# Hybrid decoder block on one core: sixteen column blocks of the input projection as block products in one stretch

## The chip, the core and the metric

The kernel runs on one core of a Trainium2 chip. A core has TensorE (PE, matrix products into PSUM), VectorE (DVE), ScalarE (ACT), GpSimd (POOL), a queue that issues DMAs (SP), and 16 DMA engines. The metric is the device time of one execution in microseconds, as a median over runs. Lower is better.

## The reference, cut to what matters

One layer with 1024 tokens and width 1024. The normed input is projected once into 5376 columns, which feed an attention branch, a recurrent branch (RWKV-7) and two gates; then come the merge, an output projection and an MLP.

```python
u = rmsnorm(h, norm1_gain)
proj = u @ w_in                                   # 1024 x 1024 times 1024 x 5376
q, k, v, r_p, k_p, v_p, w_p, a_p, g_p, gate_a, gate_b = jnp.split(proj, split_at, axis=-1)
y_attn = sliding_window_attention(q, k, v, ...) @ w_branch_attn
y_rwkv = rwkv7_time_mix(r_p, k_p, v_p, w_p, a_p, g_p, ...) @ w_branch_rwkv
mixed = jax.nn.sigmoid(gate_a) * y_attn + jax.nn.sigmoid(gate_b) * y_rwkv
h = h + mixed @ w_out
hidden = jnp.square(jax.nn.relu(rmsnorm(h, norm2_gain) @ w_ff_in))
return h + hidden @ w_ff_out

def step(S, inp):                                 # the recurrence, per head
    sa = jnp.einsum('bhij,bhj->bhi', S, a_t)
    S = S * w_t[:, :, None, :] + sa[..., None] * b_t[:, :, None, :] + v_t[..., None] * k_t[:, :, None, :]
    return S, jnp.einsum('bhij,bhj->bhi', S, r_t)
```

The recurrence runs over 1024 tokens, in eight heads of 64.

## The kernel before

Every float32 factor is split into a high and a low part (`whi`, `wlo` for weights, `uh`, `ul` for the input), and a product takes three matmuls: low by high, high by low, high by high. A split costs one ACT cast and one DVE subtraction.

**Projection blocks.** The input projection goes in blocks of 128 columns. `load_w` (L151) loads a block's weights in two halves of 256 KB and splits them; `proj` (L183) makes one half of the tokens (512) with 8x3 = 24 matmuls in a PSUM tile `ps_m`, so a block has 48. `proj_z` (L195) copies the result out and stores it in DRAM: `z_d` for the r, k and v columns of the four head pairs (12 blocks, `win_ap[8..19]`), `lz_d` for the lora columns (blocks 0 and 1). `gate` (L752) does the same through a Tanh for the 16 gate blocks (`win_ap[20..35]`), which are read again in the merge.

**Stages.** First the norm with blocks 0 and 8 (lora and the first z block). Then `phase1` (L249): z blocks 9 and 10 (`zproj(0)`), k, v and four q blocks with their preparation, then the recurrence in eight units (four head pairs, two halves of the tokens each). Each unit has three parts:
- `unit_e` prepares a unit: token shift, decay, normalisation, the small triangular inverse (a chain of short DVE instructions on `LT`). It reads `z_d` and `wa_d`.
- `unit_m` makes the unit's inverse matrices (`XT`) and `G0`; there is one `G0` buffer, so it starts when the steps of the unit before are done. Its memset of `XT` (L591) runs on POOL.
- `unit_c` (L630) runs eight steps in a chain: `ry` (PE) to `G` (DVE, L646) to `pu` (PE) to `UV` (DVE, L651) to `pd` (PE) to `sbd` (DVE, L664) to the next `ry`; then the output of the unit (`py`, group norm, `y`).

The loop at the end of `phase1` writes `unit_m(n)`, `estage(n+1)` (which is `unit_e`), `unit_c(n)`. Work that belongs to no unit is placed in the same loop: `zproj(p + 1)` with three z blocks per head pair, and by `fill(PLAN[n + 1])` the gate-lora preparation ("g", with block 1), attention blocks ("a", 8 of them, four steps each) and gates ("x", 14 of them). Two more gates (`NTAIL`) stand behind the loop, then the merge of the branches, the output projection, and the MLP. The MLP already multiplies in blocks of two by two with seven products in place of eight (`group`, `split_w`, `up`, `down`, L996).

**Order.** The order of each engine's instructions is fixed at build time by a planner. It takes, for each engine, the ready instruction with the best priority; priority is the order of the program text, moved forward by `tc.high_priority` (3000 for the three parts of a unit). So fillers go wherever the planner sees an engine free, and may run well ahead of their place in the text. At run time an engine takes its instructions strictly in that order.

Of the kernel before, what the change touches and what calls it, by code (L numbers as in the profile page):

```python
# [20 lines left out]
P = 128  # L21
D = 1024
T = 1024
# [14 lines left out]
PLAN = ("k v q q q q", "g", "a", "a", "a a", "a x", "a x x", "a x x", "a x x x x x x x x x")  # L38
NTAIL = 2

# [19 lines left out]
def hybrid_block(ctx, tc, x_ap, xt_ap, win_ap, lora_ap, wbr_ap, wout_ap, wff1_ap, wff2_ap, cst_ap,  # L60
# [10 lines left out]
    pst = ExitStack()  # L71
    pm = pst.enter_context(tc.tile_pool(name="pm", bufs=2, space=PSUM))
    ps2 = pst.enter_context(tc.tile_pool(name="ps2", bufs=2, space=PSUM))
    pqt = ExitStack()
    ps1 = pqt.enter_context(tc.tile_pool(name="ps1", bufs=1, space=PSUM, side="right"))
# [129 lines left out]

    if True:
# [34 lines left out]
    for k in range(NK):  # L241
        dump(f"uh{k}", uh[k].bitcast(F32))
# [6 lines left out]
    def phase1():  # L249
# [189 lines left out]
        def prep_g():  # L439
            proj_z([(win_ap[1], lz_d[1])])  # L440
# [295 lines left out]
        zproj(0)  # L736
        fill(PLAN[0])
        estage(0)
        for n in range(8):
# [3 lines left out]
            if hf == 0 and p + 1 < NPAIR:  # L743
                zproj(p + 1)
# [6 lines left out]

    def gate(i):  # L752
        w = load_w(win_ap[20 + i])
        for hf in range(2):
            ps = proj(w, uh, ul, hf)
            t = upool.tile([P, HALF], F32, tag="gt", name="gt", bufs=2)
            A.activation(out=t, in_=ps, func=AF.Tanh, scale=0.5)
            nc.sync.dma_start(out=gate_d[i][:, hf * HALF:(hf + 1) * HALF], in_=t)
# [174 lines left out]
    def split_w(src, pool=None, tags=("whi", "wlo")):  # L933
        hi, lo = (w_tile(F32R, t) if pool is None else pool.tile([P, NK, 128], F32R, tag=t, name=t) for t in tags)
        with tc.high_priority(offset=HP_F):
            A.copy(out=hi, in_=src)  # L936
            V.tensor_sub(out=lo, in0=src, in1=hi.bitcast(F32))  # L937
        return hi, lo

    w0 = split_w(raw["a11"], hp, ("c21", "c22"))  # L940
# [51 lines left out]
    def group(out, pairs, start):  # L992
        n, last = 0, 3 * len(pairs) - 1
        for (lh, ll), (rh, rl) in pairs:
            for a, b in ((ll, rh), (lh, rl), (lh, rh)):
                PE.matmul(out=out, lhsT=a, rhs=b, start=start and n == 0, stop=n == last, skip_group_check=True)  # L996
                n += 1
# [213 lines left out]
```

## Time and profile before

| | us |
|---|---|
| median of 3 runs | 1529.18 (1528.53 to 1529.93) |
| profiled execution | 1529.62 |
| its span, first to last instruction | 1527.8 |
| PE busy | 1491.3 (98%) |
| PE weight loads busy | 1177.2 (77%) |
| DVE busy | 1044.1 (68%) |
| ACT busy | 639.1 (42%) |
| POOL busy | 192.2 (13%) |

Busy shares are averages over stages. The span has these: norm and first blocks to 77.8 us, k, v and q to 152, the recurrence with fillers to 586, the rest of attention with gates to 642, gates alone to 706, then the merge, the output projection and the MLP to the end. A matmul's record is longer than its share of the engine, since matmuls overlap; what one costs is read from a stretch of many.

### The profile page before, as it was taken

The page shows a single profiled execution, that of the slowest core. Times are in us where ns is not written, and L with a number is a line of the kernel's source. Part 1 is how long each engine was busy: PE and PEld are TensorE (multiplying, and loading weights), DVE is VectorE, ACT ScalarE, POOL GpSimd, SP SyncE. Part 2 cuts the span into 40 slices and gives each one's busy share as a digit, 9 for nine tenths or more (in the row PEclk, how much of TensorE's full clock was granted, in tenths as well). Part 3 has the DMA queues.
Part 4 walks back from the last instruction along what each step waited for, and adds up shares of the span by engine and source line. Part 5 has one row for each costly group of instructions (what it writes and reads, how often), then busy time and mean ns, then how long its engine had stood idle before and what let it go on. Part 6 is the DMA issues. An engine that isn't in the chain of part 4 may idle for free.

```text
span 1527.8 us, 22206 instructions
## 1 busy us (share of the span) xinstructions
PE 1491.3 (98%) x8396; PEld 1177.2 (77%) x8396; DVE 1044.1 (68%) x2056; ACT 639.1 (42%) x1126; POOL 192.2 (13%) x116
## 2 busy tenths in 40 slices
PE   5999999999999999999999999999999999999998
PEld 5878777777777777788888787878787878787776
DVE  4232678888988875353656579595858687776867
ACT  6332436456545665441224354332424333423332
POOL 1000000000000000000000111323223232323230
PEclk9999999999999999999999999999999999999999
DMA  5455334334222323383433111111120111111112
GB/s 192 165 149 146 109 103 149 103 104 120 88 90 66 103 84 124 117 295 113 136 125 146 42 42 56 56 42 69 42 69 28 69 42 65 46 56 42 56 55 111
DMA packets 99771, 145.65 MB, mean 95 GB/s; under 512 B 26448, under 2 KB 48848, under 8 KB 99664
## 3 DMA queue, kind: packets, MB, share of 16 engines
q1 hardware_dynamic: 99664, 144.23, 28.8%
q8 instruction: 66, 1.08, 0.3%
q14 instruction: 41, 0.34, 0.1%
HBM read 108.54 MB, written 35.65 MB: 94 GB/s over the span
## 4 chain that ended last, share of the span: by engine, by line
PE 75%; DVE 19%; ACT 3%; issue 2%; DMA 1%; SPq 0%; DVEq 0%; ACTq 0%
PE ps_m L164 32%; PE psy L996 15%; PE psx L996 12%; DVE wlo L937 4%; DVE c L1021 2%; DVE c L1001 2%; DVE tlo L1032 2%; PE po L164 2%; PE ps_o L927 1%; PE pu L170 1%; DVE h L1094 1%; ACT c L1004 1%; ACT whi L936 1%; PE pk L246 1%; PE ps_s L170 1%
## 5 line engine op out<-in xcount | busy, mean ns | idle before, releaser
L164 PE MATMUL ps_m<-uh,wlo 128*128 128x512 f32 x576 | 235.5, 409 | 0.0
L164 PE MATMUL ps_m<-ul,whi 128*128 128x512 f32 x576 | 234.3, 407 | 0.0
L164 PE MATMUL ps_m<-uh,whi 128*128 128x512 f32 x576 | 233.0, 404 | 0.0
L996 PE MATMUL psy<-T,whi 128*128 128x512 f32 x512 | 159.6, 393 | 0.0
L164 PEld LDWEIGHTS ps_m<-uh,whi 128*128 128x128 f32 x576 | 108.6, 189 | 21.2 <-issue 0.8
L164 PEld LDWEIGHTS ps_m<-uh,wlo 128*128 128x128 f32 x576 | 108.6, 189 | 21.1 <-issue 0.6
L164 PEld LDWEIGHTS ps_m<-ul,whi 128*128 128x128 f32 x576 | 108.7, 189 | 20.2 <-issue 0.7
L996 PEld LDWEIGHTS psy<-T,whi 128*128 128x128 f32 x512 | 96.1, 188 | 21.9
L157 DVE TENSOR_TENSOR wlo<-wraw,whi 128x512 fp32r<-128x512 f32 x101 | 67.9, 687 | 56.6 <-ACT whi L156 56.4
L996 PE MATMUL psx<-tlo,whi 128*128 128x512 f32 x256 | 101.9, 398 | 4.5 <-DVE tlo L1032 4.5
L937 DVE TENSOR_TENSOR wlo<-fraw_a,whi 128x1024 fp32r<-128x1024 f32 x47 | 66.0, 1405 | 57.5 <-ACT whi L936 57.5
L936 ACT CAST whi<-fraw_a 128x1024 fp32r<-128x1024 f32 x47 | 49.3, 1049 | 129.1 <-PE psy L996 85.7
L996 PE MATMUL psx<-thi,wlo 128*128 128x512 f32 x256 | 101.6, 398 | 1.5 <-DVE h L1094 0.9
L996 PE MATMUL psx<-thi,whi 128*128 128x512 f32 x256 | 101.0, 395 | 0.0
L996 PE MATMUL psy<-T,wlo 128*128 128x512 f32 x256 | 100.6, 393 | 0.0
L967 POOL TENSOR_TENSOR fraw_a<-fraw_a,fraw_a 128x1024 f32<-128x1024 f32 x16 | 45.5, 2846 | 346.7 <-DVE s L942 345.5
L1094 DVE TENSOR_TENSOR h<-h,psx 128x1024 f32<-128x1024 f32 (+1 forms) x66 | 76.8, 1179 | 9.6 <-PE psx L996 9.6
L996 PE MATMUL psy<-tlo,whi 128*128 128x512 f32 x192 | 77.2, 402 | 3.1 <-DVE tlo L1032 3.1
L156 ACT CAST whi<-wraw 128x512 fp32r<-128x512 f32 x105 | 61.0, 619 | 45.4 <-PE ps_m L164 45.3
L996 PE MATMUL psy<-thi,wlo 128*128 128x512 f32 x192 | 75.8, 395 | 0.0
L996 PE MATMUL psy<-thi,whi 128*128 128x512 f32 x192 | 75.8, 395 | 0.0
L996 PE MATMUL psy<-B,whi 128*128 128x512 f32 x240 | 74.8, 393 | 0.0
(298 smaller groups left out, 3227.1 us busy)
## 6 DMA issues: line engine op xcount, KB each, us to landing
wraw<-win SPq DMA_DIRECT2D x72, 256.0 KB, 3.3
fraw_a<-wff SPq DMA_DIRECT2D x32, 512.0 KB, 3.2
wraw<-wff SPq DMA_DIRECT2D x32, 512.0 KB, 3.2
gate_d<-gt SPq DMA_DIRECT2D x32, 256.0 KB, 2.0
z_d<-zt SPq DMA_DIRECT2D x24, 256.0 KB, 2.3
xt<-x SPq DMA_DIRECT2D x8, 512.0 KB, 5.7
la<-wa_d SPq DMA_DIRECT2D x8, 512.0 KB, 4.3
aq<-q_d SPq DMA_DIRECT2D x8, 512.0 KB, 4.2
```

Of the source, the lines that this page charges most:

```text
L156: A.copy(out=hi[:, ks], in_=raw[:, ks])
L157: (eng or V).tensor_sub(out=lo[:, ks], in0=raw[:, ks], in1=hi[:, ks].bitcast(F32))
L164: PE.matmul(out=out, lhsT=a, rhs=b, start=(n == 0), stop=(n == last))
L170: after = PE.matmul(out=out, lhsT=lhsT, rhs=rhs, start=start, stop=stop).ins
L936: A.copy(out=hi, in_=src)
L937: V.tensor_sub(out=lo, in0=src, in1=hi.bitcast(F32))
L967: G.tensor_sub(out=a21, in0=a11, in1=a21)
L996: PE.matmul(out=out, lhsT=a, rhs=b, start=start and n == 0, stop=n == last, skip_group_check=True)
L1001: V.scalar_tensor_tensor(out=c, in0=c, scalar=0.0, in1=r2[:, (lo_, hi_)[hf]].unsqueeze(1).broadcast_to([P, 2, HALF]), op0=ALU.max, op1=ALU ...
L1021: V.tensor_sub(out=C[out], in0=C[a], in1=C[out])
L1032: V.tensor_sub(out=lo, in0=src, in1=hi.bitcast(F32))
L1094: V.tensor_add(out=ht, in0=ht, in1=ps[:, c0 % 2:c0 % 2 + step])
```

## The change

Sixteen of the blocks no longer go through `proj`. They are taken in four groups of four blocks (`GROUPS`): z blocks 9 and 10 with lora block 1 and z block 11; z blocks 12 to 15; z blocks 16 to 19; gates 2 to 5 (blocks 22 to 25). A group is a product of two by two blocks (512 weight rows by 256 columns each, against 512 input rows by 512 tokens), made from seven products P1 to P7 of 24 matmuls in place of 192 matmuls. The weights of a group come in four tiles of 512 KB from a new input `wst`. Sums of weights are made on DVE (`weight`), sums of the input once, on DVE and POOL (`in_sums`), and the products are added up on DVE (`product`). Results go to the same places in DRAM (`out_`).

The stretch stands between the norm stage and `phase1`; gates 0 and 1 go ahead of it as ordinary blocks. The PSUM pools are closed for it and opened again behind it (`psum_pools`). `phase1` loses both uses of `zproj` and block 1 in `prep_g`; `PLAN` keeps eight attention blocks and the gates 6 to 13.

```diff
-PLAN = ("k v q q q q", "g", "a", "a", "a a", "a x", "a x x", "a x x", "a x x x x x x x x x")
+PLAN = ("k v q q q q", "g", "a", "a", "a a", "a x", "a x", "a x", "a x x x x x")
+GROUPS = ((9, 10, 1, 11), (12, 13, 14, 15), (16, 17, 18, 19), (22, 23, 24, 25))
...
+    strassen_order = ("P1", "P5", "P6", "P2", "P7", "P3", "P4")
+    def split_w(src, pool=None, tags=("whi", "wlo"), hp=0):
+        hi, lo = (w_tile(F32R, t) if pool is None else pool.tile([P, NK, 128], F32R, tag=t, name=t) for t in tags)
+        with tc.high_priority(offset=hp):
+            A.copy(out=hi, in_=src)
+            V.tensor_sub(out=lo, in0=src, in1=hi.bitcast(F32))
+        return hi, lo
...
+    def in_sums(wp):
...
+        for k in range(4):
+            E.append(wp.tile([P, 2, HALF], F32, tag=f"c{k}", name=f"e{k}"))
+            for i in range(2):
+                G.tensor_add(out=E[k][:, i], in0=uh[k + 4 * i][:, lo_].bitcast(F32),
+                             in1=ul[k + 4 * i][:, lo_].bitcast(F32))
+        for k in range(4):
+            S.append(wp.tile([P, 2, HALF], F32, tag=f"sm{k}", name=f"s{k}"))
+            for i in range(2):
+                V.tensor_add(out=S[k][:, i], in0=uh[k + 4 * i][:, hi_].bitcast(F32),
+                             in1=ul[k + 4 * i][:, hi_].bitcast(F32))
+        for name, out, x, y in (("T1", (E, 0), (S, 0), (E, 0)), ("T2", (E, 0), (S, 1), (E, 0)),
+                                ("T3", (S, 0), (S, 1), (S, 0)), ("T4", (E, 1), (E, 1), (E, 0))):
+            for k in range(4):
+                o, a, b = (m[k][:, i] for m, i in (out, x, y))
+                V.tensor_sub(out=o, in0=a, in1=b)
+                t = wp.tile([P, T], F32R, name=f"{name}{k}")
+                A.copy(out=t[:, lo_], in_=o)
+                V.tensor_sub(out=t[:, hi_], in0=o, in1=t[:, lo_].bitcast(F32))
...
+    def in_groups(wp, pw, B):
...
+        def weight(g, name):
+            a11, a21, a12, a22 = (raw[g, n] for n in names)
+            w = split_w({"P1": a11, "P5": raw.get("s1"), "P6": a11, "P2": a12, "P7": a21, "P3": raw.get("s4"),
+                         "P4": a22}[name])
+            if name == "P1":
+                raw["s1"] = wp.tile([P, NK, 128], F32, tag="sm0", name="s1")
+                V.tensor_add(out=raw["s1"], in0=a21, in1=a22)
+            elif name == "P5":
+                V.tensor_sub(out=a21, in0=a11, in1=a21)
+                V.tensor_sub(out=a11, in0=raw["s1"], in1=a11)
+            elif name == "P6":
+                raw["s4"] = wp.tile([P, NK, 128], F32, tag="sm1", name="s4")
+                V.tensor_sub(out=raw["s4"], in0=a12, in1=a11)
+                fetch(g + 1, "a11")
...
+        def product(g, name, w):
...
+            for a in range(2):
+                group(ps[:, a], [((hi[:, 4 * a + k], lo[:, 4 * a + k]), B[rhs[name]][k]) for k in range(4)],
+                      name in ("P1", "P5", "P2"))
...
+            if name in ("P1", "P5", "P6", "P4"):
+                C[i, hf] = wp.tile([P, 2, HALF], F32, tag=f"c{2 * i + hf}", name="cw")
+                A.copy(out=C[i, hf], in_=ps)
+            else:
+                V.tensor_add(out=C[i, hf], in0=C[i, hf], in1=ps)
+            if name in ("P2", "P7", "P3", "P4"):
+                out_(g, i, hf)
...
     nst.close()
+    wst = ExitStack()
+    wp = wst.enter_context(tc.tile_pool(name="wspool", bufs=1))
+    for i in range(2):
+        gate(i)
+    B_in = in_sums(wp)
+    pqt.close()
+    pw = [None, wst.enter_context(tc.tile_pool(name="pw1", bufs=1, space=PSUM, side="right"))]
+    pst.close()
+    pw[0] = wst.enter_context(tc.tile_pool(name="pw0", bufs=1, space=PSUM))
+    pw.reverse()
+    in_groups(wp, pw, B_in)
+    wst.close()
+    psum_pools(1)
...
         def prep_g():
-            proj_z([(win_ap[1], lz_d[1])])
...
-        def zproj(p):
-            for i in range(0 if p else 1, 3):
-                proj_z([(win_ap[8 + 3 * p + i], z_d[3 * p + i])])
-
-        cnt = {"q": 0, "a": 0, "x": 0}
+        cnt = {"q": 0, "a": 0, "x": 6}
...
         prep_wa()
-        zproj(0)
         fill(PLAN[0])
...
-            if hf == 0 and p + 1 < NPAIR:
-                zproj(p + 1)
```

## Rows read from the trace of the kernel before

**Rows 1.** The page, part 1: busy us, share of the span, instructions.
```profile
PE 1491.3 (98%) x8396; PEld 1177.2 (77%) x8396; DVE 1044.1 (68%) x2056; ACT 639.1 (42%) x1126; POOL 192.2 (13%) x116
```

**Rows 2.** Busy time by stage; columns named in the first line.
```profile
core 0: us, PE busy (x) PEld busy (x) DVE busy (x) ACT busy (x) POOL busy (x), PEclk, DMA share, GB/s
0.00:77.80 77.80, 61.38 (x288) 51.28 (x288) 29.16 (x63) 39.87 (x65) 7.57 (x19) 1.00 0.49 175
...
152.00:586.00 434.00, 428.19 (x3703) 322.11 (x3703) 358.88 (x1265) 238.59 (x575) 6.77 (x34) 1.00 0.33 103
```

**Rows 3.** The chain that ended last, in order of time: start, length, what.
```profile
642.24 207.91 PE ps_m L164 x902
```

**Rows 4.** Busy time, a stretch of the MLP's products; columns as in rows 2.
```profile
960.00:1060.00 100.00, 98.89 (x425) 79.36 (x424) 68.82 (x52) 33.30 (x33) 31.72 (x12) 1.00 0.15 53
```

**Rows 5.** Instructions on ps_m alone, by stage: PE, PEld, DVE, ACT, clock, DMA.
```profile
152.00:586.00 434.00, 243.37 (x804) 137.82 (x803) 0.00 (x0) 19.41 (x33) 1.00 0.33 103
586.00:642.00 56.00, 43.52 (x166) 29.22 (x166) 0.00 (x0) 4.13 (x7) 1.00 0.31 106
642.00:706.00 64.00, 63.92 (x274) 51.52 (x275) 0.00 (x0) 6.76 (x12) 1.00 0.66 226
```

**Rows 6.** Busy time, the units of the recurrence; columns as in rows 2.
```profile
152.00:246.30 94.30, 91.42 (x609) 66.46 (x610) 66.81 (x222) 45.32 (x95) 0.88 (x8) 1.00 0.36 111
246.30:291.50 45.20, 44.87 (x418) 32.97 (x420) 37.59 (x125) 27.35 (x67) 1.08 (x6) 1.00 0.40 128
291.50:352.90 61.40, 60.36 (x503) 45.38 (x503) 54.19 (x201) 32.74 (x81) 0.99 (x6) 1.00 0.32 95
352.90:397.30 44.40, 44.40 (x427) 33.72 (x425) 40.08 (x147) 26.57 (x63) 1.38 (x7) 1.00 0.39 121
397.30:445.10 47.80, 46.86 (x439) 35.41 (x439) 43.06 (x148) 26.00 (x62) 0.84 (x4) 1.00 0.36 107
445.10:489.50 44.40, 44.30 (x423) 33.29 (x423) 39.71 (x140) 24.83 (x57) 0.98 (x5) 1.00 0.21 64
489.50:537.50 48.00, 47.50 (x458) 36.57 (x456) 41.09 (x156) 27.43 (x78) 0.64 (x2) 1.00 0.31 89
537.50:576.00 38.50, 38.48 (x386) 30.18 (x383) 28.16 (x100) 22.68 (x62) 0.00 (x0) 1.00 0.29 96
```

**Rows 7.** Timeline of POOL, one of six such memsets: start, length, what, [idle before].
```profile
445.12 0.53 POOL L591 MEMSET XT<- 128x512 f32 x1 [29.14 <-DMA XT<-lx_d]
```

**Rows 8.** Timeline, part of a step of the fifth unit.
```profile
434.02 0.28 DVE L651 COPY UV<-pu 64x128 f32<-64x128 f32 x1
...
434.82 0.38 PE L654 MATMUL pd<-UV,BKt 128*128 128x128 f32 x2
...
435.31 0.58 DVE L664 SCALAR_TENSOR_TENSOR sbd<-pd,wc,sw 64x64 f32<-64x64 f32 x2 [0.23 <-PE pd L654]
...
435.96 0.40 PE L164 MATMUL ps_m<-uh,whi 128*128 128x512 f32 x1
...
436.20 0.38 PE L644 MATMUL ry<-sbd,AR 128*128 128x128 f32 x2
436.22 0.75 DVE L422 SCALAR_TENSOR_TENSOR v<-z,vec,v 128x512 f32<-128x512 f32 x1
...
437.00 0.29 DVE L646 TENSOR_TENSOR G<-G,ry 64x128 f32<-64x128 f32 x1
```

**Rows 9.** The UV copies of the fifth and the last unit: ns min/median/max, first and last start.
```profile
L651 DVE COPY UV<-pu x8: 275/289/295, 417.5 to 445.1; 64x128 f32<-64x128 f32 x8
L651 DVE COPY UV<-pu x8: 277/289/295, 552.3 to 575.9; 64x128 f32<-64x128 f32 x8
```

**Rows 10.** Attention's last copy of a step, from 586 us on.
```profile
L395 ACT COPY ya<-po x10: 353/368/369, 587.8 to 642.3; 64x256 f32<-64x256 f32 x10
```

**Rows 11.** Groups by line, 152 to 586 us: busy us, mean ns, idle before.
```profile
L157 DVE TENSOR_TENSOR wlo<-wraw,whi 128x512 fp32r<-128x512 f32 x34 | 23.2, 684 | 0.6 <-ACT whi L156 0.6
```

**Rows 12.** The page, part 5: a sum of weights on POOL.
```profile
L967 POOL TENSOR_TENSOR fraw_a<-fraw_a,fraw_a 128x1024 f32<-128x1024 f32 x16 | 45.5, 2846 | 346.7 <-DVE s L942 345.5
```

More of the change, by code (lines that the diff above doesn't have):

```diff
@@ L204, in proj_z, with gate @@
                 nc.sync.dma_start(out=dst[:, hf * HALF:(hf + 1) * HALF], in_=t)
+    def gate(i):
+        w = load_w(win_ap[20 + i])
+        for hf in range(2):
+            ps = proj(w, uh, ul, hf)
+            t = upool.tile([P, HALF], F32, tag="gt", name="gt", bufs=2)
+            A.activation(out=t, in_=ps, func=AF.Tanh, scale=0.5)
+            nc.sync.dma_start(out=gate_d[i][:, hf * HALF:(hf + 1) * HALF], in_=t)
+    lo_, hi_ = slice(0, HALF), slice(HALF, T)
+    strassen_order = ("P1", "P5", "P6", "P2", "P7", "P3", "P4")
@@ new lines, in split_w, with group @@
+    def split_w(src, pool=None, tags=("whi", "wlo"), hp=0):
[4 more added lines that the diff above has]
+        return hi, lo
+    def group(out, pairs, start):
+        n, last = 0, 3 * len(pairs) - 1
+        for (lh, ll), (rh, rl) in pairs:
+            for a, b in ((ll, rh), (lh, rl), (lh, rh)):
+                PE.matmul(out=out, lhsT=a, rhs=b, start=start and n == 0, stop=n == last, skip_group_check=True)
+                n += 1
@@ new lines, in in_sums @@
+    def in_sums(wp):
+        B = {n: [] for n in ("T1", "T2", "T3", "T4")}
+        E, S = [], []
+        for k in range(4):
[16 more added lines that the diff above has]
+                V.tensor_sub(out=t[:, hi_], in0=o, in1=t[:, lo_].bitcast(F32))
+                B[name].append((t[:, lo_], t[:, hi_]))
+        for name, o, sl in (("B11", 0, lo_), ("B21", 4, lo_), ("B22", 4, hi_)):
+            B[name] = [(uh[o + k][:, sl], ul[o + k][:, sl]) for k in range(4)]
+        return B
@@ L750, in phase1 @@
         st.close()
[L752 to L758, printed above, removed]
     phase1()
@@ L931, in hybrid_block @@
     hp = gst.enter_context(tc.tile_pool(name="hpool", bufs=1, side="right"))
[L933 to L940, printed above, removed]
+    w0 = split_w(raw["a11"], hp, ("c21", "c22"), HP_F)
     s1 = hp.tile([P, NK, 128], F32, tag="c12", name="s1")
@@ L990, in weight @@
         return w
[L992 to L997, printed above, removed]
     def act2(c, hf):
@@ L1167, in _layout @@
     du, au, gu = f("decay_up"), f("aaa_up"), f("gate_up")
+    wst = w.reshape(2, 4, P, -1)[:, :, :, cols[np.array(GROUPS)]]
+    wst = wst.reshape(2, 4, P, len(GROUPS), 2, 2, P).transpose(3, 5, 0, 2, 4, 1, 6)
+    wst = np.ascontiguousarray(wst.reshape(len(GROUPS), 4, P, 8, P)[:, [0, 2, 1, 3]])
     lora = np.stack([np.concatenate([du, au]), gu])
```

63 lines of the change are left out of this document (51 added, 12 removed).

## Prediction

> **What bounds the kernel now.** I read the busy shares first, then the stages, then the recurrence unit by unit, then one step of it. TensorE (PE) is busy for 98% of the span [rows 1], so at first sight fewer matmuls mean less time. The stages say what that is made of [rows 2]. Once the input is there, up to 152 us, and from 642 us on PE works through projections without a gap; 902 of them in a row take 207.91 us, 0.2305 us each [rows 3]. Between 152 and 586 us runs the recurrence, eight units (four head pairs, two halves each). There PE is also full, but 804 of its 3703 matmuls are projections (ps_m) that have nothing to do with the unit being worked on [rows 5]: z columns for later pairs, the gate-lora block, gates. At 0.2305 us they are 185 us of the 434. They are fillers: PE does them while the chain of the recurrence waits for VectorE (DVE), ScalarE or a DMA. So the question here is not how many matmuls there are but how long the recurrence is without them.
>
> The units are marked by a memset on POOL that waits for the last step of the unit before [rows 7]; by these marks the periods are 45.2, 61.4, 44.4, 47.8, 44.4 and 48.0 us, then 38.5 for the last [rows 6]. DVE is busy for 90% of the third, fourth and fifth of these and for 73% of the last one, which alone has no following unit to prepare. A step of the chain goes pd (PE), sbd (DVE), ry (PE), G (DVE), pu (PE), UV (DVE). In [rows 8] UV starts at 434.02 and lasts 0.28, and pd starts only at 434.82, behind three fillers; sbd ends near 435.89 and ry starts at 436.20, behind one; ry is through near 436.6 and G waits until 437.00, behind a 0.75 us DVE instruction of the next unit's preparation. Both engines delay the chain, and a step takes (445.1-417.5)/7 = 3.9 us; in the last unit, with PE just as full and DVE freer, (575.9-552.3)/7 = 3.4 [rows 9].
>
> **The change, part by part.** All sums are against the profiled execution, 1529.62 us with a span of 1527.8, so 1.8 us outside it; the median is 1529.18, 0.4 lower.
>
> *Front swap.* z blocks 1 and 2 leave the stretch ahead of 77.8 us, gates 0 and 1 come in: 96 matmuls against 96, nothing.
>
> *New stretch.* Four groups of seven products of 24 matmuls, 672 for 768. The stage that works in the same product form runs 425 matmuls in 100 us, 0.2353 each with its own stalls [rows 4]: 158 us. Added to that is the hand-over of PSUM and SBUF at both ends, which no row shows. It lies between nothing (two banks are free before the last eviction) and one eviction with its store, some 6 us, since k's first projection is queued behind it on PE and v and q behind that; I take 4, nearest to the idle that the product stage shows per 100 us (1.1). Together 162 us. The sums of the input cost DVE 40 instructions at 684 ns [rows 11], 27 us, and POOL eight of half the 2846 ns form [rows 12], 11 us. They lie beside the two gates (22 us of PE) and the first products, and need only the input that exists by about 40 us; nothing, or, with that cover gone, up to 10 us for the first two sums. Per group seven splits and seven sums go to DVE, some 18 of 40 us, as in the product stage, and SP carries 512 KB weight loads in place of 256 KB ones: hidden.
>
> *What leaves.* Between 152 and 706 us there are 804+166+274 = 1244 recorded projections, 1248 by count (10 z and lora blocks, 16 gates of 48). 480 stay, 768 go: 177 us of PE. So the stage of 554 us could fall to 377 if PE stayed full, and the kernel gains by 554-377-162 = 15 us. It breaks even where the stage takes 392 us.
>
> *What the stage takes instead.* Ten blocks leave with 20 DVE splits of 684 ns [rows 11], 1.7 us per unit. (ACT loses as many casts and as many evictions; it is busy for 239 of 434 us [rows 2] and binds nowhere. SP loses 20 loads and 20 stores there, and gets 16 larger loads and 32 stores in the stretch.) DVE is busy about 40 us in a full period [rows 6]; 38.3 at the same 90% is a period of 42.5. The delay by fillers, about half a microsecond per step in [rows 8], points the same way (3.9 to 3.4, or 4 us per unit). The 61.4 us period, in which the preparation of unit 2 came late behind its own z blocks, and the 48.0 become 42.5 as well. The bounds are 38.5 (the last unit) and 45. The first unit, 94.3 us with DVE at 71%, is a chain of small work and DMA round trips: 88, between 80 and 94. The last period stays at 38, the output of the last unit at 10, from its last step [rows 9] to 586 us. Recurrence: 88+6x42.5+38+10 = 391 us for 434.
>
> Behind it, before, ten of 32 attention steps were left, at one step every 6 us (587.8 to 642.3 [rows 10]), and gates filled PE around them and until 706. Attention is filler too and needs the DVE that the recurrence needs. It can start some 60 us earlier in the first unit, as no z blocks stand ahead of it, but the rest is shorter; I take six steps left, 36 us (between 10 and 56). The two tail gates (22 us) fit beside them. Then the last attention block must be stored, loaded and split before the merge: 6 us with no gate left to hide it (0 to 11). The eight gates in the plan are low priority, and whether they run early or late does not alter the chain.
>
> Stage: 391+36+6 = 433 us, so 121 less; the new stretch costs 162. Result +41: 1527.8+41+1.8-0.4, rounded 1570 us.
>
> A rule of the Trainium skill speaks against the change: Perfetto Trace Analysis, § Optimization Strategy, says that where the most-contended engine changes between regimes, interleaving the regimes can help. The change takes two interleaved regimes apart. The trace agrees as far as [rows 2] show both engines full in one stage (PE 428 and DVE 359 of 434 us); the sum above does not use the rule.
>
> **The rivals.**
>
> *Fillers set the pace (faster).* The order on each engine is fixed when the program is built, and in [rows 8] PE matmuls that could wait stand ahead of chain matmuls twice in one step. If that is most of why a step takes 3.9 us, the freed recurrence runs at 36 us per unit or less: 88+7x36+10 = 350, attention ends beside it, and the stage meets PE's own bound, 377: 1514 us. The point is a period of 36 with a tail of 42 us, or 39.5 with one of 17. Against it: no period in the trace is under 38.5, and that one had DVE at 73%.
>
> *Between.* Periods of 39 to 41 and attention mostly done: a stage of 395 to 415, 1530 to 1550.
>
> *DVE has the last word (slower still).* The work does not fall, periods stay at 45 and all ten attention steps remain: 94+6x45+38+10+56+11 = 479, 1616 us.
>
> *A lower clock.* The granted clock is 1.00 in every stretch shown [rows 2, 6]. In all but the first of them PE is over 95% busy; in the first, ahead of 77.8 us, it is busy for 79%, still at 1.00, which speaks against this rival, though there the idle time lies mostly before the first matmul. After the change PE has at most 434-185+88 = 337 us of work (the 88 for eight gates) in 391. If the granted clock fell to the lower level (1.2 GHz) in the recurrence, three matmul groups per step and four per unit preparation would each lengthen by some tenths of a microsecond, 20 to 60 us in all: 1590 to 1630. The Trainium skill, TensorE: Matmul & The Clock Gate, Part 1, says that the array runs at half rate by default and at full rate only while it is kept busy. By that rule the recurrence would be where it falls; no row here shows it, and the forecast does not contain it.
>
> *It doesn't do what it says.* The count (96 matmuls fewer) follows from the loops; I give this no chance.
>
> **How the numbers follow.** Forecast (1550 to 1595): 0.56. Fillers set the pace, 1510 to 1526: 0.15. Between, 1526 to 1550: 0.16, of which 0.04 lies within 0.2% of 1529.2. DVE or clock, over 1595: 0.13. About 0.2%, 3 us, is what a measurement of this kernel can tell from no change. So faster 0.15, same 0.04, slower 0.81. The range goes from the PE bound, 1514, to near the upper sum, 1612; the forecast's own is 1550 to 1595.
>
> **What would show it.** Right: the stretch with products lasts about 162 us with PE full; POOL's marks in the recurrence are 41 to 44 us apart with DVE at 88 to 92%; PE there is clearly under 90% busy and waits for DVE; attention runs on after the last unit with few ps_m beside it. Wrong: marks under 38 us apart, or PE still full to the end of attention (fillers set the pace); granted clock under 1.00 in the recurrence; a product stretch over 170 us, in which case the hand-over or the input sums were not hidden.

## Result, and the profile after

The change makes the kernel slower: 1637.79 us (median of 4 runs, 1633.61 to 1639.25) against 1528.87 for the kernel before, a ratio of 1.0705 [1.0689, 1.0721]. The forecast was 1570 with a range to 1612; the sign was right and the size was not, by 68 us.

The profiled execution has a span of 1637.4 us. Two lines of its page, to be read beside [rows 1], first the busy shares, then TensorE's granted clock in 40 slices of 41 us:

```profile
PE 1529.0 (93%) x8300; PEld 1209.8 (74%) x8300; DVE 1116.4 (68%) x2120; ACT 661.8 (40%) x1130; POOL 205.2 (13%) x124
...
PEclk9999998957778999998599999999999999999999
```

There are 96 matmuls fewer (8396 to 8300 recorded), and PE is busy for 38 us more. The second line says where: the clock dips in slice 7 (the hand-over from the stretch to k), in slices 9 to 13 (the first units of the recurrence) and in 19 and 20 (the way into the merge). Before, it was 1.00 everywhere it was looked at [rows 2, 6].

The same by stage: the new stretch, k/v/q, the first unit, the seven others by their last step, the rest of attention, the start of the merge. Columns: window, length, busy us (and count) of PE, its weight loads, DVE, ACT, POOL, then granted clock, DMA share, GB/s.

```profile
71.00:229.30 158.30, 157.87 (x687) 128.75 (x686) 69.33 (x61) 47.94 (x53) 0.00 (x0) 1.00 0.26 95
229.30:322.50 93.20, 85.84 (x391) 68.34 (x389) 26.68 (x69) 26.88 (x49) 2.35 (x12) 0.93 0.55 153
322.50:440.10 117.60, 91.72 (x545) 68.55 (x546) 82.89 (x308) 64.02 (x160) 0.87 (x8) 0.67 0.33 101
440.10:488.70 48.60, 41.96 (x370) 33.09 (x372) 36.15 (x132) 24.11 (x57) 1.09 (x6) 0.72 0.22 67
488.70:548.10 59.40, 53.54 (x463) 41.32 (x463) 51.82 (x186) 32.74 (x84) 0.97 (x6) 0.91 0.35 107
548.10:595.20 47.10, 46.82 (x443) 35.46 (x441) 43.38 (x154) 27.48 (x65) 1.23 (x7) 1.00 0.33 100
...
738.00:777.70 39.70, 37.34 (x334) 29.40 (x335) 26.53 (x93) 23.82 (x67) 0.00 (x0) 0.87 0.18 64
777.70:797.00 19.30, 2.98 (x37) 2.42 (x37) 6.66 (x21) 2.70 (x5) 0.00 (x0) 0.50 0.24 83
797.00:818.00 21.00, 11.04 (x20) 5.31 (x21) 13.45 (x12) 7.31 (x7) 0.00 (x0) 0.58 0.88 310
```

Before, the same stages are, in one line each: k/v/q 82.0 us, first unit 93.4, the seven others together, the tail:

```profile
71.00:153.00 82.00, 81.72 (x398) 65.44 (x396) 25.27 (x67) 22.99 (x44) 0.10 (x1) 1.00 0.54 147
153.00:246.40 93.40, 90.52 (x608) 66.08 (x609) 65.91 (x220) 45.40 (x95) 0.94 (x9) 1.00 0.35 111
246.40:575.90 329.50, 326.56 (x3018) 247.33 (x3016) 283.75 (x1010) 187.40 (x465) 5.83 (x26) 1.00 0.33 100
575.90:705.50 129.60, 128.80 (x645) 102.91 (x646) 54.25 (x145) 59.65 (x140) 0.00 (x0) 1.00 0.49 167
```

Four marks divide the time in every kernel below: the first `th` activation (the recurrence begins), the last `UV` copy of the eighth unit, the merge's first matmul, the end. "Recurrence" is first `th` to last `UV`, "stage" is first `th` to the merge's first matmul, "rest" is from there to the end of the last instruction that counts as busy work.

| kernel | us | first th | first unit | recurrence | stage | rest |
|---|---|---|---|---|---|---|
| before | 1528.9 | 153.0 | 93.4 | 423.0 | 552.6 | 819.0 |
| after | 1637.8 | 322.5 | 117.6 | 455.2 | 474.5 | 837.4 |
| plain | 1648.5 | 330.8 | 117.4 | 455.6 | 474.9 | 838.1 |
| minus10 | 1491.9 | 152.4 | 116.0 | 454.8 | 518.1 | 818.8 |
| minus10_warm | 1529.0 | 153.5 | 90.2 | 420.4 | 551.7 | 818.9 |
| nofill | 1651.1 | 151.2 | 119.5 | 493.3 | 677.3 | 818.8 |
| warm | 1657.9 | 322.0 | 90.9 | 422.9 | 495.5 | 836.5 |
| warm8 | 1654.3 | 320.9 | 91.3 | 438.1 | 489.6 | 838.2 |
| noattn | 1640.8 | 323.5 | 104.8 | 457.0 | 476.5 | 836.8 |
| early | 1668.7 | 324.3 | 110.6 | 463.7 | 506.4 | 836.9 |
| hold3 | 1655.9 | 318.0 | 117.9 | 467.0 | 510.3 | 820.4 |
| g1 | 1553.9 | 209.5 | 94.3 | 426.7 | 510.9 | 830.8 |
| gates6 | 1560.8 | 220.7 | 92.5 | 423.2 | 497.9 | 837.3 |
| g1g | 1556.9 | 218.9 | 92.4 | 421.7 | 495.6 | 836.3 |

So after against before is +169.5 in front, -78.1 in the stage, +18.4 in the rest: 109.8 by the trace, 108.9 by the medians. 768 matmuls, 177 us at 0.2305, left the stage, and less than half of that time came back. The recurrence didn't shorten; it grew by 32 us.

Those 32 us aren't spread evenly: 24 of them lie in the first unit, ahead of its first step. From the first `th` to the first `UV` copy it is 90.9 us for 67.2 before; the eight steps take 26.7 for 26.2. More attention lies there too. A step of attention ends with one `ya` copy: the first unit holds nine of them, for one before, and the whole recurrence all 32, for 21. Both kinds of copy in the first unit, before and then after (ns min/median/max, first and last start, shapes):

```profile
L395 ACT COPY ya<-po x1: 366/366/366, 237.2 to 237.2; 64x256 f32<-64x256 f32 x1
L651 DVE COPY UV<-pu x8: 277/289/296, 220.2 to 246.4; 64x128 f32<-64x128 f32 x8
```

```profile
L533 ACT COPY ya<-po x9: 365/366/367, 335.6 to 439.2; 64x256 f32<-64x256 f32 x9
L788 DVE COPY UV<-pu x8: 281/288/295, 413.4 to 440.1; 64x128 f32<-64x128 f32 x8
```

### The profile page after: what moved, and what is told of

It reads as the page before. It is cut to its first block, busy times and chain, and to the rows that moved or that the text cites. A ratio compares the mean times of both kernels' runs of the same rounds, so it can differ in the third digit from the quotient of the medians.

```text
span 1637.4 us, 22102 instructions
## 1 busy us (share of the span) xinstructions
PE 1529.0 (93%) x8300; PEld 1209.8 (74%) x8300; DVE 1116.4 (68%) x2120; ACT 661.8 (40%) x1130; POOL 205.2 (13%) x124
## 4 chain that ended last, share of the span: by engine, by line
PE 35%; DVE 12%; ACT 2%; issue 2%; DMA 1%; ACTq 0%; DVEq 0%
PE psy L233 14%; PE psx L233 11%; PE ps_m L169 9%; DVE wlo L226 3%; DVE c L1128 2%; DVE c L1108 2%; DVE tlo L1139 2%; PE ps_o L1049 1%; DVE h L1201 1%; ACT c L1111 1%; ACT whi L225 1%; DVE c L1176 1%; DVE c L1172 1%; DMA gg<-g_d 0%; DMA yt<-ya_d 0%
## 5 line engine op out<-in xcount | busy, mean ns | idle before, releaser
L169 PE MATMUL ps_m<-uh,wlo 128*128 128x512 f32 x320 | 134.1, 419 | 2.5 <-DVE wlo L162 2.5
L169 PE MATMUL ps_m<-ul,whi 128*128 128x512 f32 x320 | 133.7, 418 | 0.0
L169 PE MATMUL ps_m<-uh,whi 128*128 128x512 f32 x320 | 132.4, 414 | 0.0
L233 PE MATMUL psw<-T,whi 128*128 128x512 f32 x256 | 79.0, 390 | 0.0
L169 PEld LDWEIGHTS ps_m<-uh,wlo 128*128 128x128 f32 x320 | 61.9, 194 | 13.9 <-DVE wlo L162 2.9
L1138 ACT CAST thi<-c 128x1024 fp32r<-128x1024 f32 x56 | 58.7, 1048 | 32.2 <-DVE c L1128 31.9
L169 PEld LDWEIGHTS ps_m<-uh,whi 128*128 128x128 f32 x320 | 61.9, 193 | 11.7 <-issue 0.2
L169 PEld LDWEIGHTS ps_m<-ul,whi 128*128 128x128 f32 x320 | 62.0, 194 | 11.1 <-issue 0.9
```

The costliest lines, as they stand in the source:

```text
L169: PE.matmul(out=out, lhsT=a, rhs=b, start=(n == 0), stop=(n == last))
```

## The experiments

Three theories stood at the start. A: PE without projections between the chain's small matmuls loses its clock, and that lengthens the chain. B: the load of DVE and attention sets the length of a unit. C: matmuls that stand ahead of the chain's own slow it.

**warm: the kernel after, with the missing PE work put back as matmuls that nothing reads.**

```diff
+    def warm(n):
+        for j in range(n):
+            ps = pm.tile([P, HALF], F32, tag="m", name="ps_w")
+            sl = slice(j % 2 * HALF, (j % 2 + 1) * HALF)
+            mm3(ps, [((uh[k][:, 0:128], ul[k][:, 0:128]), (uh[k][:, sl], ul[k][:, sl])) for k in range(NK)])
...
         def prep_g():
+            warm(2)
...
+            if hf == 0 and p + 1 < NPAIR:
+                warm(6)
```

> The changed kernel with 480 matmuls added in the recurrence, at the places where the ten blocks stood before. They multiply slices of the input by each other into PSUM and nobody reads the result, so TensorE is given back its filler without a split, a copy or a DMA; the output is the same. Theory A (the granted clock, low from 315 to 490 us and at the entry of the merge, makes the first units long): the clock returns to 1.00, the stretch from the first tanh of unit 0 to POOL's first mark falls from 118 us to about 95, the marks at 488 and 548 come 45 us apart, and the total falls by 40 us or more, to 1590 or less. Theory B (VectorE's queue sets the units, filler or not): the clock returns, the first stretch gives back at most 10 us, the marks stay 47 us apart, 1615 to 1635. Theory C (matmuls standing ahead of the chain slow it): slower than 1640.

Measured: 1657.9 us, ratio 1.0842 [1.081, 1.0873]. The recurrence is 422.9, that of the kernel before to 0.1 us, though no work was added but that of PE. The window view of its first unit and of the seven others:

```profile
322.00:412.90 90.90, 88.94 (x613) 64.77 (x612) 63.70 (x206) 38.99 (x82) 1.40 (x9) 1.00 0.27 84
412.90:744.90 332.00, 328.19 (x2998) 249.10 (x2998) 277.07 (x1004) 174.71 (x445) 5.12 (x25) 0.99 0.25 77
```

Against the kernel after, the first unit is 27 us shorter, at a clock of 1.00 for 0.67. But the planner, with PE full, also put attention elsewhere: the first unit holds one of its steps and no longer nine, as in the kernel before, and the first step of the unit comes 65.7 us after the first `th`:

```profile
L539 ACT COPY ya<-po x1: 365/365/365, 406.4 to 406.4; 64x256 f32<-64x256 f32 x1
L795 DVE COPY UV<-pu x8: 272/288/295, 387.7 to 412.9; 64x128 f32<-64x128 f32 x8
```

So warm shows that the missing PE work is what lengthened the recurrence, but not by itself whether through the clock or through the place of attention. The total missed theory A's 1590 by 68 us and lies where theory C had it: attention was pushed behind the recurrence (its last copy starts at 808.8, for 775.7), so the stage is 495.5 for 474.5. A shorter recurrence that is paid with pushed work wins nothing.

**noattn: the kernel after without attention** (zeros are stored in its place).

```diff
-                for g in range(2):
-                    pend.append(attn_s(blk, hh, g))
-                    if len(pend) > 1:
-                        attn_o(pend.pop(0))
+                ya = ap.tile([P, 2, 128], F32, tag="ya", name="ya")
+                G.memset(ya, 0.0)
+                nc.sync.dma_start(out=ya_d[:, 2 * hh:2 * hh + 2, b * 128:(b + 1) * 128], in_=ya)
```

> The changed kernel without the attention steps; zeros are stored in their place, so VectorE loses about 5 to 10 us of work in each unit and 19 us in the first, TensorE and ScalarE lose theirs too. Theory B (VectorE's load sets the period): the marks on POOL come about 41 us apart in place of 47, the first stretch falls from 118 to under 100 us, total 1560 to 1585. Theory A (clock): with still less work on TensorE the clock falls further, the first units stay long, total 1610 or more. If the dependence chain of a unit itself takes 45 us, the marks stay at 45 to 47 and the total is 1600 to 1630.

Measured: 1640.8 us, ratio 1.073 [1.0699, 1.0761]; the recurrence is 457.0. The first unit, and the last two, which have neither attention nor projections beside them:

```profile
323.50:428.30 104.80, 71.48 (x435) 51.27 (x434) 66.22 (x208) 39.06 (x72) 2.41 (x13) 0.66 0.29 89
...
678.80:736.00 57.20, 35.86 (x304) 27.11 (x305) 31.67 (x103) 10.66 (x26) 0.65 (x2) 0.56 0.10 24
736.00:780.50 44.50, 29.52 (x263) 22.21 (x263) 17.36 (x55) 8.41 (x23) 0.00 (x0) 0.50 0.02 7
```

In the last one DVE is busy for 17.36 of 44.50 us, nothing competes with the chain, and it still takes longer than the last unit of the kernel before (38.5 us with DVE at 28.16 [rows 6]). So B doesn't explain this unit. DVE's load isn't without effect, though. Units 4 to 6 run at a clock of about 1.00 with and without attention; they take 137.9 us here and 142.1 in the kernel after, 4 us less for 11 us less of DVE's work (noattn, then after):

```profile
540.90:678.80 137.90, 134.06 (x1220) 96.47 (x1218) 115.91 (x373) 61.69 (x131) 2.94 (x14) 0.99 0.25 79
548.00:690.10 142.10, 141.05 (x1321) 106.23 (x1323) 127.23 (x453) 82.01 (x198) 3.40 (x15) 1.00 0.30 92
```

And the first unit is 13 us shorter than after's at about the same clock (0.66 for 0.67), all of it ahead of the first step, which comes 76.8 us after the first `th`, for 90.9:

```profile
L784 DVE COPY UV<-pu x8: 282/289/295, 400.3 to 428.4; 64x128 f32<-64x128 f32 x8
```

So at the low clock the nine attention steps cost the first unit 13 us, about half of what it had grown by. Theory B had it under 100 us, and theory A had it stay long: it lies between. The later units, which lost attention as fill too, gave the 13 us back.

**minus10: the kernel before without ten of its blocks, and without the stretch.** The nine z blocks of the later pairs and lora block 1 aren't computed; all pairs read the columns of the first blocks.

```diff
         def prep_g():
-            proj_z([(win_ap[1], lz_d[1])])
...
-            if hf == 0 and p + 1 < NPAIR:
-                zproj(p + 1)
```

> The kernel before with the ten blocks of the recurrence simply left out (every head pair reads the z columns of the first pair, the gate lora those of the other lora); no new stretch, gates and attention as before. It is the removal alone. If units run faster without filler, as I forecast (periods of 42.5 us), the stage from 152 us to the merge meets TensorE's own bound of 443 us: 1418 us, periods 42 or less. Theory B (VectorE sets the units): periods stay at 44 to 47, gates are used up as filler, the stage takes 470 to 500 us and the total is 1445 to 1475. Theory A adds a low clock in the first unit, and then the total lies at the upper end or above it.

Measured: 1491.9 us, ratio 0.9757 [0.972, 0.9793]. Ten blocks are 480 matmuls, 110.6 us of PE, and leaving them out altogether is worth 37; my own forecast for this run, 1418 us with periods of 42 or less, missed by 74. The recurrence (454.8) is that of the kernel after (455.2) without anything of the stretch: what lengthens it is that the blocks left the recurrence, with all that the planner then moved: here too the first unit holds nine attention steps and the recurrence all 32.

**minus10_warm: the same with 480 matmuls that nothing reads in the blocks' places**; `warm` as above, in the old places of `proj_z` and `zproj`.

> The kernel before without the ten blocks (the four pairs read the first blocks' columns, as in the run without them), and in their places 480 matmuls of the same size whose results nothing reads: TensorE is busy as before, but there are no weight fetches, splits, evictions and stores. Clock theory: the recurrence is back at 423 us, against 455 without the matmuls, and the whole kernel is at 1529, give or take 8: TensorE's work is the whole of the difference of 37 us between the kernel before and the one without the blocks. Rival (the ten blocks cost by their evictions, stores and splits on VectorE and ScalarE): the recurrence stays under 423 and the kernel ends at 1492 to 1515. If PE's work comes in full on top of 1492 (110 us at full clock for 480 matmuls), 1600.

Measured: 1529.0 us, ratio 1.0004 [0.9993, 1.0015], as the clock theory had it. The work that this kernel has and minus10 hasn't is PE's alone: no weight fetch, split, copy or store. The order differs further: with the PE work back, the planner again puts one attention step in the first unit and 21 in the recurrence. The first unit and the seven others, of minus10:

```profile
152.40:268.50 116.10, 91.28 (x547) 68.66 (x548) 82.96 (x308) 63.94 (x160) 0.91 (x9) 0.68 0.33 102
268.50:607.10 338.60, 324.72 (x2951) 248.81 (x2950) 281.69 (x1007) 187.07 (x470) 5.84 (x26) 0.94 0.29 87
```

and of minus10_warm:

```profile
153.50:243.70 90.20, 88.68 (x613) 64.83 (x612) 63.56 (x207) 39.11 (x82) 1.40 (x9) 1.00 0.27 85
243.70:573.90 330.20, 326.45 (x2998) 247.79 (x2999) 276.74 (x1004) 174.94 (x445) 5.12 (x25) 1.00 0.26 77
```

Two readings. More work on PE made the recurrence 34 us shorter, with the clock at 1.00 for 0.68 and 0.94 and with eleven attention steps fewer in it. And against the kernel before, which has its attention in the recurrence in the same number (21 steps), the ten blocks' twenty splits and all their copies are gone from DVE and ACT, and the recurrence is 420.4 for 423.0: that relief is worth 2.6 us, not the 42 that the prediction gave it.

**nofill: minus10 with every gate block held behind the last unit.**

```diff
-                    gate(i)
+                    with tc.issue_after(held[0]):
+                        gate(i)
```

> The kernel before without the ten blocks, and with all gate blocks held until the last unit's output matmul, so that the recurrence has no projection work at all beside attention in its early units (the four pairs read the first blocks' columns). Clock theory: the units that have nothing beside them run at a granted clock of 0.5 to 0.6 and steps of 3.8 to 4.1 us, so first tanh to last mark is 475 to 500 us, against 455 with gates and 423 with gates and blocks, and the whole kernel is slower than the 1491.9 without the hold by more than 20 us plus the held gates that no longer hide. Rival (filler competes with the recurrence): the recurrence shortens to 390 to 440.

Measured: 1651.1 us, ratio 1.0803 [1.0762, 1.0844]; the recurrence is 493.3, within the 475 to 500 of the clock theory; the rival wanted 390 to 440.

```profile
151.20:270.70 119.50, 87.91 (x504) 65.93 (x505) 83.48 (x311) 62.01 (x156) 0.87 (x8) 0.62 0.30 90
270.70:644.50 373.80, 301.43 (x2482) 236.22 (x2483) 272.12 (x985) 169.57 (x432) 5.66 (x26) 0.63 0.19 53
```

This run parts the clock from attention, which lies as in minus10: nine steps in the first unit, 31 in the recurrence for 32. The first unit, at 0.62 for 0.68, is 3.5 us longer, and the seven others, at 0.63 for 0.94, are 35 us longer, though the gates' splits and copies are gone from DVE and ACT.

A clock of 0.63 is a mean of stretches at 1.00 (2.4 GHz) and at 0.50 (1.2 GHz). The chain's `pd` matmul shows what that is for one instruction (ns min/median/max, first and last start, shapes), first here, then in minus10_warm:

```profile
L653 PEld LDWEIGHTS pd<-UV,BKt x120: 186/331/338, 242.3 to 641.2; 128*128 128x128 f32 x120
L653 PE MATMUL pd<-UV,BKt x120: 275/421/583, 242.3 to 641.4; 128*128 128x128 f32 x120
```

```profile
L660 PEld LDWEIGHTS pd<-UV,BKt x120: 186/188/193, 219.0 to 570.9; 128*128 128x128 f32 x120
L660 PE MATMUL pd<-UV,BKt x120: 269/273/378, 219.2 to 571.0; 128*128 128x128 f32 x120
```

Weight load and matmul each take some 145 ns more. Eight steps and the unit's preparation are made of such small matmuls, each waited for: the seven later units take 373.8/7 = 53.4 us each, for 48.4 in minus10 and 47.2 in minus10_warm. From no fill to full fill the recurrence is 493.3, 455, 420 to 423; the last of these differences holds the shift of attention too.

**plain: the sixteen blocks in the same place in front, as plain block products.**

```diff
+    for i in range(6):
+        gate(i)
+    for s, d in [(win_ap[1], lz_d[1])] + [(win_ap[8 + i], z_d[i]) for i in range(1, 12)]:
+        proj_z([(s, d)])
```

> The sixteen column blocks stand in the same place in front, but as plain block products: no input sums, no sevenths, none of the new memory; the recurrence's fill is that of the kernel after. The stretch is then sixteen blocks of 48 matmuls, 16 x 48 x 0.2305 = 177 us, where the change's is 158. If the 11 us between the stretch and the k block are the hand-over of the change's memory, they are gone: first tanh at 153 + 177 = 330, against 322.5, recurrence 455, merge entry as after, and the whole kernel is at 1645, give or take 7. Rival (the seven products save what they were meant to, and the 11 us have another cause): first tanh 341, whole kernel 1656. If the block products themselves are what slows the kernel (the recurrence's length has to do with what stood in front), the recurrence is at 423 and the kernel at 1613 or less.

Measured: 1648.5 us, ratio 1.0788 [1.0757, 1.082], first `th` at 330.8, recurrence 455.6. That was foretold to within 4 us, and it splits the change in two: the move alone costs some 120 us, and the seven products give back 10.7. They save 18.7 us in the stretch (177.0 against 158.3) and lose 10.4 of that in the hand-over, so that the first `th` comes 8.3 us earlier. In the kernel after, POOL's first memset waits for the stretch's memory, and so does k's eviction on ACT, in whose queue the sum of squares `sq` then stands behind the lora preparation `lt`, which waits for a load (timelines of POOL and ACT: start, length, what, [idle before, released by]):

```profile
234.41 0.20 POOL L779 MEMSET Yt<- 64x128 f32 x1 [185.32 <-DMA gate_d<-cw]
```

```profile
235.22 0.69 ACT L422 ACTIVATE kg<-ps_m,drv 128x512 f32<-128x512 f32 x1 [2.63 <-POOL XT L728]
239.42 1.37 ACT L559 ACTIVATE lt<-z,drv 128x512 f32<-128x512 f32 x2 [3.51 <-DMA z<-lz_d]
...
243.64 0.60 ACT L424 ACTIVATE sq<-ps_m 128x512 f32<-128x512 f32 x1 [0.24 <-DVE sp_l L411]
```

In plain, `sq` follows at once, and k/v/q takes 82.8 us, for 93.2 after and 82.0 before:

```profile
254.91 0.69 ACT L296 ACTIVATE kg<-ps_m,drv 128x512 f32<-128x512 f32 x1 [3.90 <-PE ps_m L164]
255.50 0.59 ACT L298 ACTIVATE sq<-ps_m 128x512 f32<-128x512 f32 x1
```

**Three tries to mend the kernel after.** warm8 adds 192 of the reader-less matmuls, in the first unit only; early writes the kernel's own gates in earlier units; hold3 holds gates 13 to 15 until the last unit's output.

```diff
 # warm8
         def prep_g():
+            warm(2)
...
+            if n == 0:
+                warm(6)
 # early
+PLAN = ("k v q q q q x x", "g x", "a", "a", "a a x", "a x", "a x", "a x", "a x")
 # hold3
+                    (late_gate if i >= 13 else gate)(i)
```

> The kernel after, with TensorE work that nothing reads only in the thin units: the 24-matmul halves of the kernel with 480 of them, but just the two in front of the first unit and the six in it (192 matmuls). Clock theory: the first unit (first tanh to first mark) falls from 117.6 us to about 90 to 95, as with all 480, and the recurrence from 455 to about 425 to 435; as only about 22 us of TensorE work at full clock is added and it lies inside the first unit, the attention isn't pushed behind the recurrence as it was with 480, so the whole kernel is 1605 to 1620. Rival (the late units are pushed by whatever is put in front, so the added work comes back in full at the end): recurrence 423 to 455, whole kernel 1637 to 1660.

> The kernel after with its ten remaining gate blocks in other places and none added: two in front of the first unit, one each in the first, fourth, fifth, sixth, seventh and eighth, two behind. Clock theory: fill in the first unit keeps its granted clock up, the first unit falls from 117.6 us to 90 to 105 and first tanh to last mark from 455 to 430 to 445; as the last unit has less beside it, some of it is given back there; whole kernel 1615 to 1632. Rival (the length from the first tanh to the merge, 475 us, is the sum of TensorE's work in it at whatever clock, and the place of the fill is nothing): 1635 to 1645, with attention pushed towards the end as with the added matmuls.

> The changed kernel with the matmuls of gates 13, 14 and 15 held back until the last unit's output matmul, 33 us of TensorE work that would otherwise be filler within the recurrence. If filler within the recurrence is worth nothing and the entry of the merge (28 us of loads, casts and splits, one block after the other, with TensorE idle and its clock low) is exposed, the work hides the entry: the units are unchanged and the total falls by 15 to 28 us, to 1610 to 1622. If the entry is not what is late, the 33 us are simply added behind: 1640 to 1670.

Measured: 1654.3 us, ratio 1.0824 [1.0793, 1.0856]; 1668.7, 1.0921 [1.0862, 1.0979]; 1655.9, 1.0829 [1.0789, 1.0869]. All three miss their totals. In warm8 the first unit is 91.3 as foretold (117.6 in the kernel after), again with one attention step in it, and the recurrence 438.1; but 192 matmuls are 44 us at full clock, not the 22 that I wrote, and the first attention copy moved from 335.6 to 405.6 us, the last from 775.7 to 802.8. In early the gates ahead of the first unit were through by 343 us, the clock fell behind them, and the late units had nothing left (early's first unit, the seven others, attention behind them):

```profile
324.30:434.90 110.60, 103.76 (x631) 78.18 (x632) 78.43 (x274) 57.58 (x134) 1.02 (x9) 0.86 0.38 118
434.90:788.00 353.10, 317.30 (x2771) 241.45 (x2768) 276.22 (x999) 179.61 (x454) 5.75 (x26) 0.83 0.26 77
788.00:831.00 43.00, 21.95 (x103) 16.74 (x103) 15.99 (x62) 15.69 (x43) 0.00 (x0) 0.50 0.15 50
```

Fill in the wrong unit is lost twice: attention went late, and its own chain then ran alone at 0.50. In hold3 the last units slowed for want of the held gates (recurrence 467.0). What it did show is the way into the merge: with three gates left as cover the rest is 820.4 us, that of the kernel before, for 837.4. So 17 of the 18.4 us in the rest are the eight loads, sums and splits at the merge's entry, with nothing beside them (797 to 818 us after, PE busy for 11.04).

**Which part of the move costs what.** g1 keeps one group (columns 9, 10, 22, 23) and two gates in front and puts the other blocks back. gates6 moves only six gates, as plain products, and leaves every unit its fill. g1g is gates6 with four of the six gates as one group of seven products.

```diff
 # g1
+GROUPS = ((9, 10, 22, 23),)
 # gates6
+PLAN = ("k v q q q q", "g", "a", "a", "a a", "a x", "a x x", "a x x", "a x x x")
...
+    for i in range(6):
+        gate(i)
 # g1g
+GROUPS = ((22, 23, 24, 25),)
```

> The change with one group instead of four: columns 9, 10, 22 and 23 go through seven products in front, two gates go in front, and ten blocks less three are back inside the recurrence where the kernel before has them. The sum by the traces: one group saves 2 of 16 block halves of 2.8 us each in time on TensorE (about 5.5 us), the hand-over costs the 11 us seen after, two gates in front are filler lost (2 x 11.3), of which the recurrence gives back nothing if its fill was free. Recurrence theory: 423 to 430, as the units have nearly their old fill; whole kernel 1530 to 1565. Rival (the stretch itself is what costs, whatever its length: sums of the inputs, the new pools, the memory hand-over): over 1565. Faster than before (under 1526) only if the hand-over is hidden and the tail shrinks by the gates that moved.

> The kernel before with six of its sixteen gate blocks moved in front as plain products; the z columns and the fill of every unit of the recurrence stay as they were, only the tail behind the recurrence loses the six blocks. The front pays 6 x 48 x 0.2305 = 66 us, first tanh at 219. Theory (work behind the recurrence, where TensorE is the limit, comes back nearly in full; work beside the units, which fills the waits of the chain and holds the clock, doesn't): first tanh to first merge matmul falls from 552.6 by 60 to 66, first tanh to last mark stays 423 to 428, and the whole kernel is 1529 to 1538. Rival (every block moved to the front comes back at the 44% of the whole change): the stage falls by 29, whole kernel 1566.

> One part of the change alone, put where it costs least: two plain gates and one group of four gates (columns 22 to 25) through seven products in front, everything else as in the kernel before, with the fill of every unit. Against the same six gates as plain products the group saves six of 48 matmuls' halves, 24 x 2 x 0.2305 / 2 = 5.5 us on TensorE. If the stretch had no other cost it would be 5.5 us faster than the run with the six plain gates; by the 11 to 18 us that the memory hand-over took in the runs with groups, and up to 12 us more at the merge's entry, it is 5 to 25 us slower: 1538 to 1558. Faster than the kernel before (under 1526) only if the hand-over is hidden.

Measured: g1 1553.9 us, ratio 1.0167 [1.0134, 1.0201]; gates6 1560.8, 1.0214 [1.0185, 1.0244]; g1g 1556.9, 1.0189 [1.0159, 1.0218]. In all three the recurrence is 422 to 427: with its fill kept, it keeps its length. In gates6 six blocks cost 67.7 us in front (66 expected) and bring back 54.7 in the stage, 81%, where the ten blocks of minus10 brought 31%. Its total missed (1529 to 1538 expected), because of a cost that the expectation hadn't: the last gate is evicted at 705.6 and attention's last copy starts at 710.9, so the merge's entry lies bare again. Its windows, of the tail and of 21 us from the merge's first matmul:

```profile
643.90:718.60 74.70, 62.96 (x358) 49.48 (x356) 33.65 (x124) 41.09 (x113) 0.00 (x0) 0.93 0.36 122
718.60:740.00 21.40, 11.14 (x20) 5.44 (x21) 13.64 (x13) 7.29 (x7) 0.00 (x0) 0.58 0.88 303
```

67.7 - 54.7 + 18.3 = 31.3, for 32.7 measured. The group of g1g saves 3.9 us against gates6, of the 5.5 that its matmuls are. The queue at k isn't seen in g1g, where z blocks 9 and 10 stand between the stretch and k; it is in g1, where from k's eviction to DVE's use of it 15.0 us go by, for 6.1 before.

No kernel that computes everything beats the one before. A group saves 5.5 us of PE, and its place in front cost more than that each time. Groups behind the recurrence, where PE is full, weren't tried.

## Why the prediction came out wrong

By its own terms:

- *Front swap and product stretch*: right. Predicted 162 us with 4 of hand-over; the products took 158.3, as summed from [rows 4]. The input sums were hidden.
- *Hand-over*: mis-sized, 4 for 11.2 (93.2 against 82.0 for k/v/q). Its bound of 6 counted one eviction. What was late was a queue: k's work on ACT behind the lora preparation, and that behind POOL's wait for the stretch's memory. 7 us.
- *What leaves*: right, 768 matmuls. (The projection that they belong to has 36 blocks of 128 columns, so 4608 columns; the 5376 given with the reference is a slip, and nothing here rests on it.)
- *What the stage takes instead*: this step failed. It made the recurrence 381 us from the first `th` on; it is 455.2. Of the 74 us, 42 (from the 423.0 of before down to 381) are a relief of which minus10_warm shows 2.6. I had read the 90% of DVE in [rows 6] and the half microsecond of waiting in [rows 8] as a price per unit that goes when the splits and fillers go. minus10_warm takes the splits away and the recurrence is 420.4 for 423.0; noattn takes 52 of 365 us of DVE's work out of the recurrence, which stays as long (its last two units at a lower clock; at 1.00, 11 us of DVE's work were worth 4); and in the kernel after, the unit from 548.1 to 595.2 us takes 47.1 with the clock at 1.00. Most of the high busy share beside the chain was work that fitted into the chain's waits, not what it waited for.
- The other 32 came with the missing PE work: minus10 has them without the stretch, and warm has them gone. Two causes lie in them, and no run parts them wholly. One is attention, which the prediction let start 60 us earlier in the first unit and put at nothing there: the unit was to take 88 us and took 117.6. Without attention, at the same clock, it takes 104.8, so 13 of its 24 us go with the nine steps; what those would cost at 1.00 no run shows. The other is the clock: about 19 of the 32 us, if those 13 are attention's own, up to all of them, if attention costs nothing at 1.00; that a lower clock alone lengthens the units, nofill shows. It was my fourth rival, with a price of 20 to 60 us and a small chance. The price was about right; the chance was wrong. I argued from the stretch ahead of 77.8 us, where PE was busy for 79% at 1.00 [rows 2]. PE's busy share in the kernel after's first unit is about that too, 91.72 of 117.6, and the clock is 0.67: the busy share didn't tell the two apart. In the stretch ahead of 77.8 us the first matmul comes at 16.4 us, and from 20 us on PE is busy for 57.80 of 57.80, so it couldn't speak against this rival. The Trainium skill, TensorE: Matmul & The Clock Gate, Part 1, has the array at full rate only while it is kept busy; the runs agree (0.62, 0.68 and 1.00 in the first unit of nofill, minus10 and minus10_warm).
- *Tail*: 10 + 36 + 6 = 52 us predicted, 19.3 + 18.4 = 37.7 measured. Attention was done with the last unit, since eleven more of its steps than before had gone into the recurrence; the merge's entry was 18 and not 6, eight blocks one behind the other rather than the last one alone.

Sum: 41 + 7 + 42 + 32 - 14 = 108, for 108.6 against the median that the forecast stood on. The rival "Fillers set the pace" didn't come true: in nofill, with no projection in the way, the units are longer, though at a lower clock. "DVE has the last word" came near in time for a wrong reason. The break-even that the prediction named, a stage of 392 us, would have needed a recurrence shorter than any kernel here has. The rule of Perfetto Trace Analysis, § Optimization Strategy, in the Trainium skill, that regimes with different busiest engines may gain by being interleaved, pointed the right way: undoing that interleaving (plain) costs some 120 us.

What stays open: what sets the 47 us of a unit at full clock. DVE's load, the splits and attention have a small part in it (2.6 us of a whole recurrence for the splits and copies, some 4 in three units for attention). How the first unit's 24 us divide between attention and the clock stays open as well: no run has nine attention steps there at a clock of 1.00. The nearest is early, with five steps at 0.86 and 110.6 us. Whether the fill's place in PE's queue costs part of it couldn't be told apart, since taking the fill away takes the clock away.

## What to carry to other kernels

Work that fills the waits of a chain costs less than its own time where it stands (here 37 us for 110.6 us of PE), and moving it in front of the chain pays its full price. Before such a move, leave the work out once: the difference is what the move can win back at most for that work. Then put it back once as work that nothing reads, to see which engine's part of it counted. Look at what the fill does besides using PE: it held the clock of the chain's own matmuls, it kept attention out of the first unit, and the last of it covered the loads of the next stage. A busy share next to a chain says that an engine has work, not that the chain waits for it. And where a planner fixes the order, count what else moved before a difference is put down to one cause.

## What the runs showed of the hardware

More TensorE work made the same recurrence shorter: 480 matmuls that nothing reads took it from 454.8 to 420.4 us, in part by moving attention, and cost 37 us in total where 110.6 us of them were added. With attention in place, taking the gates away made it longer (493.3 us in nofill for 454.8 in minus10). In nofill, at a mean clock of 0.63, a `pd` weight load and matmul have medians of 331 and 421 ns, for 188 and 273 in minus10_warm at 1.00, while the DVE copy between them doesn't change (`UV`, 288 and 289 ns). PE's busy share over nofill's recurrence is still 79%, the same as ahead of 77.8 us in the kernel before, where the clock is 1.00 [rows 2] and the idle time lies mostly before the first matmul.
